# Softmax weights of an attention layer, turned by VectorE and a trip through DRAM instead of TensorE transposes

## The chip, the cores and the metric

The kernel runs on one core of one Trainium2 chip. The metric is the device time of one execution in microseconds. The engines are called as the profile calls them: PE is TensorE (matmuls; PEld is its weight load), DVE is VectorE, ACT is ScalarE, POOL is GpSimd, SP is SyncE. POOL and SP issue most DMAs here; "SPq" and "POOLq" are their DMA queues. Each engine works off its own list of instructions in order, and an instruction that has to wait holds up everything behind it on its engine.

## The reference

Two layers of a decoder run over 512 rows of 1024 floats. Layer 0 mixes the rows by dilated attention, layer 1 by a gated linear recurrence; each mixer is followed by a gated feed-forward block with a short convolution. The change touches the attention of layer 0 alone:

```
for g in range(3):              # (window, dilation): (128, 1), (512, 4), (2048, 16)
    o[g], lse[g] = dilated_group_attention(q, k, v, bias, window, dilation)
alpha = softmax(stack(lse), axis=0)
out   = sum(alpha * o) @ w_o    # 8 heads of 128 in each group

# in one group, in blocks of window // dilation positions:
logits = q @ k.T * scale + bias;  p = exp(logits - max);  o = p @ v / sum(p)
```

To multiply the weights p by v on TensorE, p has to lie with its keys on the partitions, while the softmax needs its queries there. So every block of p is turned between the two.

## The kernel before

Every product of activations and weights is done in three passes (`mm3`, line 255): each matrix is split into a rounded part and a remainder, hi x hi, hi x lo and lo x hi. ScalarE writes the rounded part of the weights (lines 143 and 149), VectorE the remainder (lines 144 and 150), up to eight units ahead of TensorE.

Attention works through the heads in pairs. For a pair, `feat_tiles` projects queries and keys one 128-column tile after the other (24 matmuls each, rows `ps L255`); for every second pair in the first half, and for every pair in the second half, `values` projects the values (rows `v L673`). Between these tiles, a call of `tick()` takes one step of whatever side work is due. The steps of a head are written as a generator: `yield n` means that the next part is put into the program n ticks later. The whole program order is fixed in this way; nothing reorders it later.

- `local(h, ...)` is the group with dilation 1, 8 heads. It loads a bias table `T` (`toeplitz`, line 586, a DMA on GpSimd), forms the scores (S, line 724), adds the bias and takes the maximum (`scores`, line 711, VectorE), takes exponentials (line 737, ScalarE), then after 2 ticks transposes 7 blocks of 128x128 on TensorE (line 746) and copies them out of PSUM (lines 749 and 751), and one tick later multiplies them by v (O, line 759).
- `strided(h, ...)` is the other two groups together, 8 heads: two tables, S at line 774, exponentials at line 789, a normalization on VectorE (line 801), then after 2 ticks eight transposes (line 808) with copies on ScalarE (line 810). A small row of factors goes through DRAM (`crow` and `cn`, lines 813 and 815). Four ticks later (five for head 6) O follows at line 821.
- `regroup` carries the sums of the first half through DRAM once (lines 835 and 837).
- The side work `biases` writes the rows from which the tables are cut (line 579) and then runs `feature_columns`: per-feature parameters of the later layers are loaded with small DMAs on GpSimd into tiles `st` (`columns`, line 485), transposed on TensorE (line 488) and copied to tiles `cols`. It has five such groups, the first with eight loads.

Tiles `L`, `PT`, `qk`, `v`, `o0`, `cn`, `st` and others come from one pool of 28 buffers of 128x512; the bias tables have two buffers.

Of the kernel before, what the change touches and what calls it, by code (L numbers as in the profile page):

```python
# [11 lines left out]
F32 = mybir.dt.float32  # L12
F32R = mybir.dt.float32r
I32 = mybir.dt.int32
AF = mybir.ActivationFunctionType
# [3 lines left out]
P = 128  # L19
# [16 lines left out]
TOE_BUFS = 2  # L36
# [38 lines left out]
def kernel(  # L75
# [25 lines left out]
    nc = tc.nc  # L101
# [5 lines left out]
    gp = ctx.enter_context(tc.tile_pool(name="gp", bufs=GEN_BUFS))  # L107
    sp = ctx.enter_context(tc.tile_pool(name="sp", bufs=8))
    pp = ctx.enter_context(tc.tile_pool(name="pp", bufs=8, space=bass.MemoryType.PSUM))
    dp = ctx.enter_context(tc.tile_pool(name="dp", bufs=1, space=bass.MemoryType.DRAM))  # L110
# [3 lines left out]
    def nm(s):  # L114
        uid[0] += 1
        return f"{s}{uid[0]}"

    def gen(dt=F32, s="g"):
        return gp.tile([P, 512], dt, tag="g", name=nm(s))

    def psum(s="ps"):
        return pp.tile([P, 512], F32, tag="ps", name=nm(s))

    def small(cols, s="s"):
        return sp.tile([P, cols], F32, tag=f"s{cols}", name=nm(s))

    mm = nc.tensor.matmul

    ident = cp.tile([P, P], F32, tag="ident", name="ident")
# [435 lines left out]
    def attention(hT, post, pre):  # L565
# [17 lines left out]
        def toeplitz(dst, g, h, n):  # L583

            o = rowv[g].offset + h * TOE + 257 - n
            nc.gpsimd.dma_start(dst, bass.AP(tensor=rowv[g].tensor, offset=o, ap=[[1, P], [1, n]]))

        vrows = []
        st0 = cp.tile([P, 4, 2, 8], F32, tag="st0", name="st0")
        o0 = []  # L590
# [116 lines left out]
        def vtile(vs, t, part):  # L707
            return vs[t][:, part * P : (part + 1) * P]

        def scores(dst, ps, bias, mx):  # L710
            nc.vector.tensor_tensor_reduce(
                dst, ps, bias[:, ::-1], scale=1.0, scalar=3 * NEG, op0=ALU.add, op1=ALU.max, accum_out=mx
            )

        def local(h, hh, q, k, v):
            T = gp.tile([P, 256], F32, tag="toe", name=nm("toe"), bufs=TOE_BUFS)
            toeplitz(T, 0, h, 256)
            L = [gen(s="L") for _ in range(2)]
            Sp = [psum("S") for _ in range(2)]
            mx = small(4)  # L720
            for a in range(4):
                o = (a % 2) * 256
                lo, k0 = (P, 0) if a == 0 else (0, (a - 1) * P)
                mm(Sp[a // 2][:, o + lo : o + 256], q[hh][:, a * P : (a + 1) * P], k[hh][:, k0 : (a + 1) * P],  # L724
                   start=True, stop=True)
            for a in range(4):
                o = (a % 2) * 256
                lo = P if a == 0 else 0
                scores(L[a // 2][:, o + lo : o + 256], Sp[a // 2][:, o + lo : o + 256], T[:, : 256 - lo], mx[:, a : a + 1])
            neg = small(4)  # L730
            nc.vector.tensor_scalar(neg, mx, -1.0, None, op0=ALU.mult)
            nc.vector.tensor_copy(st0[:, :, 0, h], mx)
            for a in range(4):
                o = (a % 2) * 256
                lo = P if a == 0 else 0
                ls = L[a // 2][:, o + lo : o + 256]
                nc.scalar.activation(ls, ls, AF.Exp, bias=neg[:, a : a + 1], accum_out=st0[:, a, 1, h : h + 1])
            yield 2
            blocks = [(a, j) for a in range(4) for j in range(2) if a or j]
            pts = {}  # L740
            for c in range(2):
                grp = blocks[4 * c : 4 * c + 4]
                ps = psum("PT")
                for n, (a, j) in enumerate(grp):
                    o = (a % 2) * 256 + j * P
                    nc.tensor.transpose(ps[:, n * P : (n + 1) * P], L[a // 2][:, o : o + P], ident)  # L746
                pt = gen(s="PT")
                if c:
                    nc.scalar.activation(pt[:, : len(grp) * P], ps[:, : len(grp) * P], AF.Copy)
                else:  # L750
                    nc.vector.tensor_copy(pt, ps)
                for n, b in enumerate(grp):
                    pts[b] = pt[:, n * P : (n + 1) * P]
            yield 1
            po = psum("O")
            for a in range(4):
                js = [1] if a == 0 else [0, 1]
                for j in js:
                    mm(po[:, a * P : (a + 1) * P], vtile(v, a - 1 + j, h % 4), pts[a, j], start=j == js[0], stop=j == 1)  # L759
            o = gen(s="o0")  # L760
            nc.scalar.activation(o, po, AF.Copy)
            o0.append(o)

        def strided(h, hh, qks, v):
            st1 = st1_box[0]
            mx = small(12)
            Ls = []
            for gi, (q, k) in enumerate(qks):
                T = gp.tile([P, 256], F32, tag="toe", name=nm("toe"), bufs=TOE_BUFS)
                toeplitz(T[:, :P], gi + 1, h, P)  # L770
                ps = psum("S")
                for r in range(4):
                    c = slice(r * P, (r + 1) * P)
                    mm(ps[:, c], q[hh][:, c], k[hh][:, c], start=True, stop=True)  # L774
                L = gen(s="L")
                for r in range(4):
                    c = slice(r * P, (r + 1) * P)
                    scores(L[:, c], ps[:, c], T[:, :P], mx[:, 4 * gi + r : 4 * gi + r + 1])
                Ls.append(L)
            M, nM, c0, den, s12 = small(4), small(4), small(4), small(4), small(8)  # L780
            nc.vector.tensor_tensor(M, mx[:, 0:4], mx[:, 4:8], op=ALU.max)
            nc.vector.tensor_tensor(M, M, st1[:, 0, h, :], op=ALU.max)
            nc.vector.tensor_scalar(nM, M, -1.0, None, op0=ALU.mult)
            nc.vector.tensor_tensor(c0, st1[:, 0, h, :], M, op=ALU.subtract)
            nc.scalar.activation(c0, c0, AF.Exp)
            for gi, L in enumerate(Ls):
                for r in range(4):
                    c = slice(r * P, (r + 1) * P)
                    nc.scalar.activation(
                        L[:, c], L[:, c], AF.Exp, bias=nM[:, r : r + 1],  # L790
                        accum_out=s12[:, 4 * gi + r : 4 * gi + r + 1],
                    )
            nc.vector.tensor_tensor(den, c0, st1[:, 1, h, :], op=ALU.mult)
            nc.vector.tensor_tensor(den, den, s12[:, 0:4], op=ALU.add)
            nc.vector.tensor_tensor(den, den, s12[:, 4:8], op=ALU.add)
            rden = small(4)
            nc.vector.reciprocal(rden, den)
            nc.vector.tensor_tensor(c0, c0, rden, op=ALU.mult)
            for L in Ls:
                L3 = L.rearrange("p (r c) -> p r c", r=4)  # L800
                nc.vector.tensor_tensor(L3, L3, rden.unsqueeze(2).to_broadcast([P, 4, P]), op=ALU.mult)
            yield 2
            pts = []
            for L in Ls:
                ps = psum("PT")
                for r in range(4):
                    c = slice(r * P, (r + 1) * P)
                    nc.tensor.transpose(ps[:, c], L[:, c], ident)  # L808
                pt = gen(s="PT")
                nc.scalar.activation(pt, ps, AF.Copy)  # L810
                pts.append(pt)
            row = dp.tile([P, 4], F32, name=f"crow{h}")
            nc.gpsimd.dma_start(row, c0)
            cn = gen(s="cn")
            nc.gpsimd.dma_start(cn, bass.AP(tensor=row.tensor, offset=row.offset, ap=[[0, P], [1, S]]))
            yield 5 if h == 6 else 4
            po = psum("O")
            for r in range(4):
                c = slice(r * P, (r + 1) * P)
                for gi in range(2):  # L820
                    mm(po[:, c], vtile(v, r, 2 * gi + hh), pts[gi][:, c], start=gi == 0, stop=gi == 1)  # L821
            r_u = "p (u r) -> p r u"
            o = o0[h]
            nc.vector.tensor_tensor(o, o, cn, op=ALU.mult)
            nc.vector.tensor_tensor(
                o.rearrange(r_u, r=4), po.rearrange("p (r u) -> p r u", r=4), o.rearrange(r_u, r=4), op=ALU.add
            )
            oT[h] = o
# [14 lines left out]
        for hp in range(4):  # L843
            q, k = [], []
            if hp % 2 == 0:
                v = []
# [9 lines left out]
        for hp in range(4):  # L856
            qs, ks, v = [], [], []
# [209 lines left out]
```

## Time and profile before

| | |
|---|---|
| median of 3 runs | 1474.26 us (1474.23 to 1474.28) |
| the profiled execution | 1474.08 us, of which the span of the profile is 1472.3 us |
| PE busy | 1463.5 us, 99% of the span |
| DVE busy | 847.1 us, 58% |
| ACT busy | 679.6 us, 46% |
| POOL busy | 43.2 us, 3% |
| DMA | 154.39 MB, 105 GB/s on average |
| attention | from the start to about 480 us |

A row of a timeline or of the chain gives the start in us from the span's start, the duration in us, the engine, the line, the operation with output and input, and how many instructions were merged (x16). What stands in brackets at the end is the idle time of the engine before it and what ended that. A row of the groups gives busy time in us and the mean of one in ns. A row of the waits gives the total in us, how often, and the longest. A row of the DMA issues gives the size and the median time from issue to landing in us. One fp32 matmul of S or O shows as two MATMUL rows, a transpose as one.

### The profile page before, as it was taken

How to read it: one execution, taken by the hardware profiler on the slowest of the kernel's cores; microseconds unless marked ns; L12 is line 12 of the kernel's file. 1: busy time of each engine (PE TensorE's matmuls, PEld its weight loads, DVE VectorE, ACT ScalarE, POOL GpSimd, SP SyncE). 2: the span in 40 equal slices, each digit the busy share in tenths (PEclk: the TensorE clock that was granted, in tenths of full speed). 3: DMA queues.
4: the chain of work that ended last, by engine and by line, in shares of the span. 5: the costliest groups of instructions: out<-in, count | busy, mean ns of one | idle time of the engine just before them, and what ended most of it. 6: DMA issues, size and time to landing. Idle time of an engine off the chain costs nothing.

```text
span 1472.3 us, 18613 instructions
## 1 busy us (share of the span) xinstructions
PE 1463.5 (99%) x7030; PEld 1231.3 (84%) x7030; DVE 847.1 (58%) x1888; ACT 679.6 (46%) x1538; POOL 43.2 (3%) x111
## 2 busy tenths in 40 slices
PE   9999999999999999999999999999999999999998
PEld 7888888888888898888888888988898888888886
DVE  5645546454545786555555337868785555565333
ACT  7645536262615454433444234489454333444321
POOL 0400001010100000000000000000000000000000
PEclk9999999999999999999999999999999999999999
DMA  6622235343434333223223231341323323223201
GB/s 203 198 65 89 91 91 140 112 137 113 127 125 130 118 115 114 87 91 110 86 106 124 86 99 44 122 138 58 110 97 108 101 86 114 87 87 129 100 0 58
DMA packets 116082, 154.39 MB, mean 105 GB/s; under 512 B 5208, under 2 KB 97592, under 8 KB 115992
## 3 DMA queue, kind: packets, MB, share of 16 engines
q1 hardware_dynamic: 112104, 144.72, 29.9%
q0 software_dynamic: 3296, 7.43, 2.5%
q8 instruction: 55, 0.90, 0.3%
q10 hardware_dynamic: 592, 1.05, 0.2%
q14 instruction: 35, 0.29, 0.1%
HBM read 146.81 MB, written 6.38 MB: 104 GB/s over the span
## 4 chain that ended last, share of the span: by engine, by line
PE 93%; ACT 4%; DVE 3%; issue 1%; DVEq 0%; ACTq 0%
PE ps L255 54%; PE acc L255 24%; PE v L673 7%; PE v L614 1%; DVE xb L879 1%; PE O L821 1%; PE S L774 1%; PE O L759 1%; PE S L724 1%; DVE wlo L150 1%; PE tr L302 1%; ACT sig L900 1%; ACT whi L149 1%; PE PT L808 0%; PE PT L746 0%
## 5 line engine op out<-in xcount | busy, mean ns | idle before, releaser
L255 PE MATMUL ps<-hT,whi 128*128 128x512 f32 (+1 forms) x2752 | 801.6, 375 | 0.0
L255 PEld LDWEIGHTS ps<-hT,whi 128*128 128x128 f32 x2752 | 503.2, 188 | 91.0
L255 PE MATMUL ps<-hT,wlo 128*128 128x512 f32 (+1 forms) x1376 | 515.2, 374 | 0.0
L150 DVE TENSOR_TENSOR wlo<-raw,whi 128x512 fp32r<-128x512 f32 x360 | 230.8, 686 | 190.1 <-ACT whi L149 190.1
L255 PEld LDWEIGHTS ps<-hT,wlo 128*128 128x128 f32 x1376 | 259.1, 188 | 46.5
L149 ACT ACTIVATE whi<-raw 128x512 fp32r<-128x512 f32 x360 | 204.7, 622 | 135.3 <-PE acc L255 120.9
L538 DVE SCALAR_TENSOR_TENSOR u<-ps,cols,u 128x511 f32<-128x511 f32 x192 | 143.8, 749 | 139.9 <-ACT u L534 136.5
L255 PE MATMUL acc<-whi,ahi 128*128 128x512 f32 x512 | 199.9, 390 | 0.0
L255 PE MATMUL acc<-whi,alo 128*128 128x512 f32 x512 | 199.4, 389 | 0.1
L255 PE MATMUL acc<-wlo,ahi 128*128 128x512 f32 x512 | 199.2, 389 | 0.0
L143 ACT ACTIVATE whi<-raw,first_w 128x128 fp32r<-128x128 f32 (+1 forms) x432 | 146.5, 427 | 62.4 <-PE ps L255 53.2
L534 ACT ACTIVATE u<-ps,cols 128x512 f32<-128x512 f32 x96 | 74.8, 779 | 209.3 <-PE ps L255 209.3
L144 DVE SCALAR_TENSOR_TENSOR wlo<-raw,first_w,whi 128x128 fp32r<-128x128 f32 (+1 forms) x432 | 141.9, 391 | 37.5 <-ACT whi L143 37.5
L255 PEld LDWEIGHTS acc<-whi,alo 128*128 128x128 f32 x512 | 96.1, 188 | 20.3 <-DVE alo L150 0.6
L255 PEld LDWEIGHTS acc<-wlo,ahi 128*128 128x128 f32 x512 | 96.2, 188 | 19.9
L255 PEld LDWEIGHTS acc<-whi,ahi 128*128 128x128 f32 x512 | 96.2, 188 | 19.7
L673 PE MATMUL v<-whi,hT 128*128 128x512 f32 x320 | 103.6, 395 | 0.0
L673 PEld LDWEIGHTS v<-whi,hT 128*128 128x128 f32 x320 | 60.1, 188 | 12.1
L549 ACT ACTIVATE u<-u 128x512 f32<-128x512 f32 x48 | 30.3, 632 | 81.2 <-DVE u L538 81.2
L673 PE MATMUL v<-wlo,hT 128*128 128x512 f32 x160 | 62.3, 390 | 0.0
L353 DVE TENSOR_TENSOR post<-acc,gain 128x512 f32<-128x512 f32 x32 | 22.0, 686 | 46.5 <-ACT junk L262 46.5
L601 DVE TENSOR_TENSOR qk<-ps,roots 128x512 f32<-128x512 f32 x24 | 16.6, 690 | 53.4 <-PE ps L255 53.4
(163 smaller groups left out, 969.2 us busy)
## 6 DMA issues: line engine op xcount, KB each, us to landing
raw<-in_ffn_w_up_dram SPq DMA_DIRECT2D x48, 1024.0 KB, 5.2
raw<-in_attn_w_qkv_dram SPq DMA_DIRECT2D x26, 1024.0 KB, 5.0
raw<-in_ffn_w_down_dram SPq DMA_DIRECT2D x24, 1024.0 KB, 5.0
raw<-in_attn_w_qkv_dram SPq DMA_DIRECT2D x19, 512.0 KB, 6.7
raw<-in_lru_w_in_dram SPq DMA_DIRECT2D x8, 1024.0 KB, 5.4
vrows<-v SPq DMA_DIRECT2D x16, 256.0 KB, 3.8
vp<-vrows SPq DMA_DIRECT2D x16, 256.0 KB, 3.7
raw<-in_attn_w_o_dram SPq DMA_DIRECT2D x4, 1024.0 KB, 5.0
```

What stands on the lines that cost most here:

```text
L143: nc.scalar.activation(hi[:, k], raw[:, k], AF.Copy, scale=w)
L144: nc.vector.scalar_tensor_tensor(lo[:, k], raw[:, k], w, hi[:, k].bitcast(F32), op0=ALU.mult, op1=ALU.subtract)
L149: nc.scalar.activation(hi, raw, AF.Copy)
L150: nc.vector.tensor_tensor(lo, raw, hi.bitcast(F32), op=ALU.subtract)
L255: mm(dst, l[a], r[b], start=start and n == 0, stop=stop and n == 2)
L302: nc.tensor.transpose(ps[:, k * P : (k + 1) * P], xs[i][:, k * P : (k + 1) * P], ident)
L353: nc.vector.tensor_tensor(u[i], parts[i], g[:, at[i]], op=ALU.mult)
L534: nc.scalar.activation(u, ps, AF.Identity, scale=cc[:, j : j + 1], bias=cc[:, 48 + j : 49 + j])
L538: nc.vector.scalar_tensor_tensor(u[:, d:], ps[:, : S - d], wc, u[:, d:], op0=ALU.mult, op1=ALU.add)
L549: nc.scalar.activation(u, u, AF.Gelu_apprx_tanh)
L601: nc.vector.tensor_tensor(dst, src, row, op=ALU.mult)
L673: mm(banks[t], hT[a][:, k, t * P : (t + 1) * P], W[b][:, k % 2, :], start=(k, a, b) == (0, 0, 0), stop=(k, a, b) == (KD - 1, 1, 0),)
```

## The change

The transposes on TensorE, their PSUM tiles and their copies are taken out of both `local` and `strided`. In their place `turned` lets VectorE turn each 32x32 block of `L` where it is (one instruction for 3 or 4 blocks of 128x128) and writes the result to a DRAM tile; `fetched` reads it back with four DMAs, one for each group of 32 partitions, so that each 32x32 block arrives at its place in the full transpose. The columns of the fetched tile come in another order, so O reads its moving operand as four runs of 32. All these DMAs are issued by GpSimd. Per head there are two turned tiles, two writes and eight fetches.

The steps are put elsewhere too. The turning and the trip are now in the same part as the exponentials, ahead of the `yield`; O follows 4 ticks after S in `local` (3 before) and 6 in `strided` (7 for head 6), as before. `table` asks for a bias table one head ahead, and a `strided` head has both of its tables in one tile.

```
+        def table(strided, h, take=True):
+            if (strided, h) not in tables:
+                T = gp.tile([P, 256], F32, tag="toe", name=nm("toe"), bufs=TOE_BUFS)
+                for i in range(1 + strided):
+                    n = 256 >> strided
+                    toeplitz(T[:, i * n : i * n + n], i + strided, h, n)
+                tables[strided, h] = T
+            return tables.pop((strided, h)) if take else None

+        def turned(L, n, name, first=0):
+            T = gen(s="T")
+            nc.vector.transpose(
+                T[:, : n * P].rearrange("p (c n j) -> p c n j", c=4, j=32),
+                L[:, first * P : (first + n) * P].rearrange("p (n c j) -> p c n j", c=4, j=32),
+            )
+            d = dp.tile([P, n * P], F32, name=nm(name))
+            nc.gpsimd.dma_start(d, T[:, : n * P])
+            return d

+        def fetched(d, n):
+            pt = gen(s="PT")[:, : n * P]
+            for c in range(4):
+                nc.gpsimd.dma_start(
+                    pt[32 * c : 32 * c + 32].rearrange("j (b x) -> j b x", b=4),
+                    d.rearrange("(b j) (c x) -> c j b x", j=32, c=4)[c],
+                )
+            pt = pt.rearrange("p (b n i) -> p n b i", b=4, i=32)
+            return [pt[:, i] for i in range(n)]

         def local(h, hh, q, k, v):
-            T = gp.tile([P, 256], F32, tag="toe", name=nm("toe"), bufs=TOE_BUFS)
-            toeplitz(T, 0, h, 256)
+            T = table(0, h)
...
                 nc.scalar.activation(ls, ls, AF.Exp, bias=neg[:, a : a + 1], accum_out=st0[:, a, 1, h : h + 1])
-            yield 2
+            table(*((0, h + 1) if h < 7 else (1, 0)), False)
+            ds = [turned(L[c], 4 - (c == 0), "ptl", int(c == 0)) for c in range(2)]
             blocks = [(a, j) for a in range(4) for j in range(2) if a or j]
-            pts = {}
-            for c in range(2):
-                grp = blocks[4 * c : 4 * c + 4]
-                ps = psum("PT")
-                for n, (a, j) in enumerate(grp):
-                    o = (a % 2) * 256 + j * P
-                    nc.tensor.transpose(ps[:, n * P : (n + 1) * P], L[a // 2][:, o : o + P], ident)
-                pt = gen(s="PT")
-                if c:
-                    nc.scalar.activation(pt[:, : len(grp) * P], ps[:, : len(grp) * P], AF.Copy)
-                else:
-                    nc.vector.tensor_copy(pt, ps)
-                for n, b in enumerate(grp):
-                    pts[b] = pt[:, n * P : (n + 1) * P]
-            yield 1
+            pts = dict(zip(blocks, fetched(ds[0], 3) + fetched(ds[1], 4)))
+            yield 4
             po = psum("O")
...
         def strided(h, hh, qks, v):
+            T = table(1, h)
             for gi, (q, k) in enumerate(qks):
-                T = gp.tile([P, 256], F32, tag="toe", name=nm("toe"), bufs=TOE_BUFS)
-                toeplitz(T[:, :P], gi + 1, h, P)
...
-            yield 2
-            pts = []
-            for L in Ls:
-                ps = psum("PT")
-                for r in range(4):
-                    c = slice(r * P, (r + 1) * P)
-                    nc.tensor.transpose(ps[:, c], L[:, c], ident)
-                pt = gen(s="PT")
-                nc.scalar.activation(pt, ps, AF.Copy)
-                pts.append(pt)
+            if h < 7:
+                table(1, h + 1, False)
+            ds = [turned(L, 4, "pts") for L in Ls]
             row = dp.tile([P, 4], F32, name=f"crow{h}")
             nc.gpsimd.dma_start(row, c0)
+            pts = [fetched(d, 4) for d in ds]
             cn = gen(s="cn")
             nc.gpsimd.dma_start(cn, bass.AP(tensor=row.tensor, offset=row.offset, ap=[[0, P], [1, S]]))
-            yield 5 if h == 6 else 4
+            yield 7 if h == 6 else 6
...
-                    mm(po[:, c], vtile(v, r, 2 * gi + hh), pts[gi][:, c], start=gi == 0, stop=gi == 1)
+                    mm(po[:, c], vtile(v, r, 2 * gi + hh), pts[gi][r], start=gi == 0, stop=gi == 1)
```

In the changed file the lines of `local` and `strided` stand some lines further down: S is at 757 and 794, O at 780 and 835, the turning at 730, the write at 735 and the fetch at 742; `toeplitz`, `columns` and `mm3` keep theirs.

More of the change, by code (lines that the diff above doesn't have):

```diff
@@ L586, in toeplitz @@
             nc.gpsimd.dma_start(dst, bass.AP(tensor=rowv[g].tensor, offset=o, ap=[[1, P], [1, n]]))
+        tables = {}
+        def table(strided, h, take=True):
[6 more added lines that the diff above has]
+            return tables.pop((strided, h)) if take else None
         vrows = []
@@ L777, in strided @@
                     c = slice(r * P, (r + 1) * P)
-                    scores(L[:, c], ps[:, c], T[:, :P], mx[:, 4 * gi + r : 4 * gi + r + 1])
+                    scores(L[:, c], ps[:, c], T[:, gi * P : gi * P + P], mx[:, 4 * gi + r : 4 * gi + r + 1])
                 Ls.append(L)
```

## The prediction

> **What bounds the kernel now.** I read the page first, then what TensorE waited for, then the chain of waits in the attention stretch, and last the timelines of GpSimd and ScalarE around the one place where the changed order of instructions looked dangerous.
>
> ```profile
> span 1472.3 us, 18613 instructions
> PE 1463.5 (99%) x7030; PEld 1231.3 (84%) x7030; DVE 847.1 (58%) x1888; ACT 679.6 (46%) x1538; POOL 43.2 (3%) x111
> PEclk9999999999999999999999999999999999999999
> PE 93%; ACT 4%; DVE 3%; issue 1%; DVEq 0%; ACTq 0%
> ```
> ```profile
> PE warm L995 <- DVE one L1027: 1.5, 1, 1.5
> ```
>
> TensorE (PE) is busy 99% of the span and 93% of the chain that ends last. The second fence is the longest of its waits in the view; the others it lists are of 0.2 us. So two things count: TensorE work that is taken out comes off the end, and a wait that TensorE is given is paid in full, because no slack follows it. VectorE (58%) and ScalarE (46%) have room.
>
> **What is removed.** The chain's pieces show what the transposes hold on TensorE's path.
>
> ```profile
> 74.31 0.20 PE cols L488
> 74.51 0.91 PE PT L746 x7
> ...
> 82.66 0.76 PE PT L746 x7
> ...
> 237.62 0.87 PE PT L808 x8
> ```
>
> The 56 transposes of `local` (8 heads of 7) are eight pieces, the first of 0.91 and seven like the second row, 0.76 to 0.77: 6.3 us. The 64 of `strided` (8 heads of 8) are eight pieces like the third row, 0.87 or 0.88: 7.0 us. The gain on the path is 13.3 us. The copies out of PSUM that go with them, 24 on ScalarE and 8 on VectorE, are off the path, since nothing on TensorE waits for them above 0.2 us; I count them at nothing.
>
> **What VectorE gets.** 32 block transposes of 384 or 512 columns. No trace row shows one. The nearest are a 128x512 copy and, as the slow end, the add that writes every fourth element:
>
> ```profile
> L751 DVE COPY PT<-PT 128x512 f32<-128x512 f32 x8 | 5.5, 688 | 15.2 <-PE PT L746 15.2
> L825 DVE TENSOR_TENSOR o<-O,o 128x512 f32<-128x512 f32 x8 | 8.6, 1069 | 5.5 <-PE O L821 5.4
> ```
> ```profile
> 65.48 1.42 DVE L144 SCALAR_TENSOR_TENSOR wlo<-raw,first_w,whi 128x512 fp32r<-128x512 f32 x2 [2.58 <-ACT whi L143]
> ```
>
> I take 0.65 us, next to the copy's 0.69 (1069 ns is the other end), since runs of 32 elements stay contiguous. In `local` the new pass must wait for the exponentials, and VectorE's queue behind it holds the weight splits of L144; but those wait for the same stretch of ScalarE today (2.58 us idle), so the pass falls into idle time. In `strided` it follows VectorE's own normalization and adds 1.3 us per head, under eight weight units split ahead. Cost on the path: none. Without that cover it would be 32 x 0.65 - 5.5 = 15 us; at 1069 ns, 29 us.
>
> **What GpSimd gets, and what it is queued ahead of.** This decides the sign. Each head now issues two writes to DRAM and eight fetches on GpSimd's queue, in order. In the built program of the changed kernel GpSimd's order is: table of head 0, table of head 1, the ten DMAs of head 0, table of head 2, the ten of head 1, and only then the L485 loads of `columns`. On TensorE the place of the first L488 transpose, which needs eight of those loads, is unchanged. Before, the loads went out early:
>
> ```profile
> 48.99 2.02 POOL L485 DMA_DIRECT2D st<-in_lru_conv_w_dram  x4
> ...
> 52.48 0.50 POOL L485 DMA_DIRECT2D st<-in_lru_lambda_dram  x1
> ```
>
> They were out at 53 us and TensorE asked at 74.3: over 20 us of lead. Now they stand behind two trips that cannot start until heads 0 and 1 have their exponentials:
>
> ```profile
> 63.66 0.18 ACT L737 ACTIVATION_READ_ACCUMULATOR L<-L,s 128x1 f32 x1
> 64.65 0.18 ACT L737 ACTIVATION_READ_ACCUMULATOR L<-L,s 128x1 f32 x1
> 71.66 0.18 ACT L737 ACTIVATION_READ_ACCUMULATOR L<-L,s 128x1 f32 x1
> ```
> ```profile
> vrows<-v SPq DMA_DIRECT2D x16, 256.0 KB, 3.8
> cn<-crow POOLq DMA_DIRECT2D x8, 256.0 KB, 4.5
> toe<-rowv POOLq DMA_DIRECT2D x16, 64.0 KB, 3.1
> crow<-s POOLq DMA_DIRECT2D x8, 2.0 KB, 1.9
> st<-in_lru_conv_w_dram POOLq DMA_DIRECT2D x4, 4.0 KB, 2.4
> st<-in_lru_conv_b_dram POOLq DMA_DIRECT2D x1, 4.0 KB, 5.3
> st<-in_lru_lambda_dram POOLq DMA_DIRECT2D x1, 4.0 KB, 4.4
> L586 POOL DMA_DIRECT2D toe<-rowv x24 | 12.9, 539 | 290.1 <-DVE s L711 198.3 <-DVE st L732 90.4 <-DVE s L781 1.4
> L835 POOL DMA_DIRECT2D strows<-st x1 | 0.8, 772 | 31.3 <-ACT L L737 31.3
> ```
> ```profile
> 453.66 0.54 POOL L813 DMA_DIRECT2D crow<-s  x1 [4.06 <-DVE s L798]
> 455.86 0.54 POOL L815 DMA_DIRECT2D cn<-crow  x1 [1.66 <-DMA crow<-s]
> ```
>
> A 256 KB write on GpSimd's queue isn't in the trace. `vrows` has its size and direction (3.8), `cn` its size and queue (4.5); I take the middle, 4.15, with ends 1.9 (`crow`) and 4.5. The next issue comes 2.2 us after `crow` where 1.9 is the landing: 0.3 more. An issue of 128 strips takes 0.54 (L586), and a fetch has 128 strips; the end above is 0.77 (L835, 512 strips).
>
> On the clock of the profile before: head 0's first half has its exponentials at 63.8, is turned at 64.4 and issued. It is back for reading at 64.4 + 4.15 + 0.3 = 68.85; the second half, written at 65.5, is ready under the first four fetches. Eight fetches of 0.54 end at 73.2, the table at 73.7. Head 1 was turned by 71.84 + 0.65 = 72.5, so its writes wait for the queue: issued 73.7 and 74.2. Its first half is ready at 78.15, its fetches end at 82.5. Eight column loads of 0.50 follow; the last issues at 86.0 and lands 4.4 later, at 90.4. TensorE stands at L488 from 74.3 to 90.4: **16.1 us**, once. The other column loads follow on at 0.5 us and are there when asked, one and two tiles later.
>
> By the Trainium skill, page "DMA: Bandwidth & Descriptors", section "Anatomy of one DMA — SWDGE (gpsimd) path", a DMA issued by GpSimd takes about 2.0 us plus its bytes over 436 GB/s, so an estimate of 2.5 us for the 192 KB write and 2.0 for a column load: a stop of about 10 us instead of 16.1, and 1472.5 us for the whole. Its 2.2 us for 64 KB stands against a measured 3.1, its 2.6 us for 256 KB against 4.5, so the rows decide.
>
> **What the stop does to the rate behind it.** The trace shows TensorE after a rest only at the start:
>
> ```profile
> 1.47 2.50 PE L995 MATMUL warm<-one 128*128 128x512 f32 x5 [1.47 <-DVE one L1027]
> 4.87 1.48 PE L995 MATMUL warm<-one 128*128 128x512 f32 x3
> 7.47 1.00 PE L614 MATMUL v<-wlo,hT 128*128 128x512 f32 x2
> 10.62 1.07 PE L614 MATMUL v<-whi,hT 128*128 128x512 f32 x4
> ```
>
> Five matmuls in 2.50 us are 0.53 apart (less 0.39 for the last one's length), four in 1.07 us are 0.23: half rate, although the PEclk row says 9 there. From 4.87 to the end of the third row TensorE worked 3.6 us almost unbroken and stayed slow; half of that is lost, **1.8 us**. Ends: 0, if a rest in mid-run does nothing, and 3.4, half of 1.47 to 8.3. The Trainium skill, "TensorE: Matmul & The Clock Gate", Part 1, states the rule against any such stop: after an idle window of about 3.4 us the clock is halved until a window of work has passed, 1.7 us lost as an estimate; the start-up rows agree, and no run shows it after a mid-kernel stop.
>
> **Edits at nothing.** The tables are asked for earlier, but no score waits for one (L711's releaser in the groups is the S matmul), so nothing is gained. The O matmuls of `local` come one tick later, those of `strided` at the same tick. They now read 4 runs of 32 columns; no matmul in the trace reads its moving side so, and I count no cost. The trips move 448 KB per `local` and 512 KB per `strided` head each way, some 15 MB over 400 us, 38 GB/s. The tightest trip is head 7's:
>
> ```profile
> 453.25 1.78 PE S L774 x16
> ...
> 478.64 3.57 PE O L821 x32
> 463.17 1.28 DVE L801 TENSOR_TENSOR L<-L,s 128x512 f32<-128x512 f32 x2
> ```
>
> Head 7's weights are normalized 11.2 us after its S began (464.45). Two transposes of head 6 ahead and one of its own make 13.1; written and readable at 17.5; eight fetches issued by 21.8, the last landing at 24.4. Its O comes, without the transposes, 25.4 - 1.75 + 1.78 = 25.4 us after S. The margin is 1 us: nothing now, up to 3 us if landing or issuing is slower.
>
> **The sum.** -13.3 + 16.1 + 1.8 = +4.6 us. Against the profiled execution (1472.3 us of span, 1474.08 in all) that is 1478.7; the median of the runs is 0.18 above that execution, so the forecast is **1478.9**. About 0.2% (2.9 us) is what a measurement of this kernel can tell from no change; +4.6 is 0.31%.
>
> **The rivals.**
> - *Short trips: faster or no change.* Small transfers on this queue land in 1.9 and 2.4 us. With these, head 0's fetches end at 70.6, head 1's writes wait for its own exponentials (the second at 72.5, the first 1.1 earlier, as in head 0), its fetches end at 77.6, the last load issues at 81.1 and lands at 83.5. The stop is 9.2 us: 1470.2 without a slow restart, 1472.0 with it. It becomes a gain when the stop and its restart are under 13.3. The skill's DMA rule above would give about this case. Against it: every 64 to 256 KB transfer took 3.1 to 4.5, and of the loads the four later ones 4.4 to 5.3. Chance 0.2, of which 0.09 passes 0.2%.
> - *GpSimd's queue becomes the bound.* At 0.77 an issue 16 fetches before the loads cost 3.7 us more, at 4.5 and 5.3 us the landings 1.6 more: a stop of 21.4, a restart of 3.4, and heads 6 and 7 late by 3: +14.5, 1488.8. It shows where an O matmul waits for PT. For it: the queue is in order and the margin is 1 us; against: 0.54 for 128 strips is steady over 24 issues. Chance 0.22.
> - *Broken-up reads slow the O matmuls.* The add with broken-up access takes 1069 ns against the copy's 688. The 240 passes of the O matmuls (112 and 128), 0.111 us each by the 478.64 row, at that ratio would cost 15 us: 1494. Chance 0.05, since runs of 128 bytes are left.
> - *The change does what it says but nothing waits*, 1461.0: only if the column loads were ahead in GpSimd's queue, and the built order has them behind. Chance 0.02.
>
> **How the numbers follow.** The forecast, a stop of 13 to 19 us with a short restart, has 0.51 and runs from 1476 to 1482. Of it 0.15 lies within 0.2%, together with 0.11 of the short trips: same 0.26. Faster: 0.09, the other part of the short trips with the last rival inside it. Slower: 0.65. The range goes from 1472.5, inside the short trips, to 1489.0, the queue rival.
>
> **What would show it.** Right: TensorE's waits of after have one entry of 13 to 19 us at L488, released by the loads into `st`, and GpSimd shows the L485 rows after 80 us; the first matmuls behind it stand 0.4 to 0.5 us apart; elsewhere attention is shorter by 0.76 or 0.87 per head. Wrong: no wait at L488, waits of TensorE at the O matmuls (L780, L835) in many heads, block transposes over 1.1 us with splits late behind them, or fetches that occupy GpSimd for over 0.8 us.

## The result, and the profile after

The changed kernel takes 1485.37 us in the median (1484.73 to 1486.44, 4 runs) against 1474.26 (1474.23 to 1474.28) before: the ratio is 1.0076, with a 95% interval of 1.0064 to 1.0088. It is slower by 11.1 us, 0.8%. The forecast was 1478.9, on the right side and 6.5 us too low. The profiled execution took 1486.44 us, 12.4 more than the profiled one of before; all sums below are made against these two.

The page of the changed kernel, the same lines as before:

```profile
span 1484.7 us, 18710 instructions
PE 1456.8 (98%) x6910; PEld 1223.1 (82%) x6910; DVE 860.3 (58%) x1912; ACT 669.7 (45%) x1514; POOL 131.5 (9%) x271
PEclk9989999999999899999999999999999999999999
PE 82%; ACT 5%; issue 5%; DVE 4%; DMA 3%; POOL 1%; DVEq 0%; ACTq 0%; POOLq 0%
```

TensorE has 120 instructions less, as the change says. Its share of the chain that ends last fell from 93% to 82%, and in two slices the granted clock has a dip where the row of before was flat. The waits of TensorE say where (total, times, longest, in us):

```profile
PE cols L488 <- DMA st<-in_lru_lambda_dram: 14.1, 1, 14.1
PE O L835 <- DMA PT<-pts: 4.8, 2, 2.8
PE O L835 <- DMA vp<-vrows: 0.4, 1, 0.4
```

There are two stops: the one at the first column transpose, which was forecast, and one at an O near the end of attention, which was not.

**The first stop.** The chain that ended last, from 74 us on:

```profile
74.74 1.09 DMA ptl<-T
75.84 2.79 issue
78.62 1.40 POOL PT L742 x3
...
83.00 3.50 POOL st L485 x7
86.50 1.64 DMA st<-in_lru_lambda_dram
88.14 0.30 issue
88.44 0.34 PE cols L488
88.78 7.72 PE ps L255 x24
```

Read from below: TensorE goes on at 88.44 because the eighth column load has landed. That load was issued at 86.50, behind seven others on GpSimd's queue, which had begun at 83.00, behind the fetches of head 1, which had begun at 78.62, behind its own writes. For the 2.79 us called `issue` the profile names no releaser; in the program the fetches have to wait there for these writes to land. It is the round trip of another head that stands ahead of the loads. Behind the stop, the next tile of 24 matmuls takes 7.72 us, where the same tile takes 5.6 at full rate (experiment 3).

**The second stop.** TensorE's timeline around the O matmuls of heads 6 and 7 in the second half, and GpSimd's before it (start, duration; in brackets the idle time ahead and its end):

```profile
481.48 1.50 PE L835 MATMUL O<-PT,vp 128*128 128x128 f32 x12
483.38 0.71 PE L835 MATMUL O<-PT,vp 128*128 128x128 f32 x4 [0.40 <-DMA vp<-vrows]
486.90 0.76 PE L835 MATMUL O<-PT,vp 128*128 128x128 f32 x2 [2.82 <-DMA PT<-pts]
489.68 3.33 PE L835 MATMUL O<-PT,vp 128*128 128x128 f32 x14 [2.01 <-DMA PT<-pts]
```
```profile
471.69 1.09 POOL L735 DMA_DIRECT2D pts<-T  x2
472.77 0.54 POOL L826 DMA_DIRECT2D crow<-s  x1
476.99 4.38 POOL L742 DMA_DIRECT2D PT<-pts  x8 [3.68 <-issue]
```

Head 7's last fetch is issued by 481.4 and is still awaited at 489.7, 8 us later. The same stretch in windows (PE busy, PEld, DVE, ACT, POOL; then the granted clock, the DMA engines' share, and GB/s):

```profile
480.00:485.00 5.00, 3.69 (x24) 3.03 (x22) 1.93 (x3) 0.00 (x0) 1.94 (x4) 1.00 1.02 272
485.00:490.00 5.00, 1.08 (x3) 0.85 (x4) 0.18 (x1) 0.63 (x1) 0.00 (x0) 0.56 1.08 298
490.00:495.00 5.00, 5.00 (x20) 4.52 (x20) 2.48 (x4) 0.63 (x1) 0.00 (x0) 0.50 0.93 321
```

The DMA engines are full from 480 to 490 while TensorE waits, and behind the wait its clock is granted at half. This slows the O matmuls themselves: the 14 rows from 489.68 to 492.66 are 0.21 us apart, where the 12 rows in one piece at 481.48 are 0.11 apart.

**The sum, from one tile's start to the same tile's start in both traces.** The first stop with its neighbours puts TensorE 14.2 us behind, the half-rate tile another 2.1; the block without transposes takes back 6.3 in the first half and 7.0 in the second; the O of the last pair takes 11.2 us (481.48 to 492.66) where 3.5 was due, 7.7 too many, of which 5.2 are waits and 2.5 slow or broken-up matmuls, and the slow matmuls behind it cost 1.5. That is 14.2 + 2.1 - 6.3 - 7.0 + 7.7 + 1.5 = 12.2, and from 513 us on the two traces run in parallel, 12.2 us apart.

### The profile page after: what moved, and what is told of

Same layout as the page of the kernel before. It is cut to its first block, busy times and chain, and to the rows that moved or that the text cites. A ratio compares the mean times of both kernels' runs of the same rounds, so it can differ in the third digit from the quotient of the medians.

```text
span 1484.7 us, 18710 instructions
## 1 busy us (share of the span) xinstructions
PE 1456.8 (98%) x6910; PEld 1223.1 (82%) x6910; DVE 860.3 (58%) x1912; ACT 669.7 (45%) x1514; POOL 131.5 (9%) x271
## 3 DMA queue, kind: packets, MB, share of 16 engines
q10 hardware_dynamic: 592, 1.05, 0.2%
## 4 chain that ended last, share of the span: by engine, by line
PE 82%; ACT 5%; issue 5%; DVE 4%; DMA 3%; POOL 1%; DVEq 0%; ACTq 0%; POOLq 0%
PE ps L255 49%; PE acc L255 23%; PE v L685 6%; DMA PT<-pts 1%; ACT whi L143 1%; DVE xb L893 1%; DMA raw<-in_attn_w_qkv_dram 1%; PE O L780 1%; PE v L626 1%; DVE wlo L150 1%; DVE wlo L144 1%; PE S L794 1%; PE tr L302 1%; PE O L835 1%; ACT sig L914 1%
## 5 line engine op out<-in xcount | busy, mean ns | idle before, releaser
L685 PEld LDWEIGHTS v<-whi,hT 128*128 128x128 f32 x320 | 60.1, 188 | 12.2
```

Source lines behind the costliest of these rows:

```text
L685: mm(banks[t], hT[a][:, k, t * P : (t + 1) * P], W[b][:, k % 2, :], start=(k, a, b) == (0, 0, 0), stop=(k, a, b) == (KD - 1, 1, 0),)
```

## The experiments

Beside each of them the kernel before was run on the same chip, with a median of 1474.1 us every time.

**1. The column loads first.** All column loads are issued right behind the first two tables, ahead of any trip.

```
+                if g == 2:
+                    table(0, 0, False)
+                    table(0, 1, False)
+                    load_columns()          # the DMAs of L485, all five groups
...
-            nc.gpsimd.dma_start(st[at : at + c, :P], src)
+        st = loaded.pop(0)
```

> The column loads are issued on GpSimd right behind the first two bias tables, ahead of all trips, as in the kernel before; everything else is the changed kernel. Theory (the stop at the first column transpose, 14.1 us, and the slow tile behind it, 2.1 us, come from the place of these loads in GpSimd's queue): both go, 1485.4 - 16.3 = 1469 us, with the wait at heads 6 and 7 left. Rival (the trips load GpSimd's queue as such, and the stop only shows where it surfaces first): other waits of TensorE come up in the first half, and the time stays over 1475.

Measured: 1469.47 us (1468.04 to 1470.54, 7 runs), ratio 0.9969 (0.9958 to 0.998). The wait at `cols` is gone; of waits at O, this is the longest row:

```profile
PE O L853 <- DMA PT<-pts: 6.1, 2, 5.0
```

No other wait came up in the first half, as the rival would have it. Against the changed kernel it is 15.9 us, which is about the stop and its slow tile (14.1 + 2.1). One moved block of issues turns the sign of the whole change.

**2. The last pair on TensorE again.** Only heads 6 and 7 of the second half are transposed as before.

```
+            if h >= 6:
+                yield 2
...             # transposes on TensorE and copies on ScalarE, as before
+            else:
+                ds = [turned(L, 4, "pts") for L in Ls]
...
-            yield 7 if h == 6 else 6
+            yield (7 if h == 6 else 6) - 2 * (h >= 6)
```

> Heads 6 and 7 of the second half are transposed on TensorE again, as in the kernel before; all other heads make the trip. Theory (the last trip is late and costs 7.7 us of stop and 1.5 us of slow matmuls behind it): this goes and 1.75 us of transposes come back: 1485.4 - 9.2 + 1.8 = 1478. Rival (the DMA engines are full there whatever the weights do, and O waits for the values as well): O still waits for the values' DMA, over 1483.

Measured: 1477.79 us (1477.25 to 1478.81, 9 runs), ratio 1.0025 (1.0015 to 1.0035). This is 7.6 us under the changed kernel, about the tail's 9.2 (7.7 + 1.5) less the 1.8 that 16 transposes cost. The first stop alone is left:

```profile
PE cols L488 <- DMA st<-in_lru_lambda_dram: 13.3, 1, 13.3
```

That the time lies within 1.1 us of the forecast is in part luck: 1.8 us of transposes are back, which the forecast had removed, and the stop is 2.8 us shorter than forecast.

**3. TensorE kept busy through the first stop.** Sixty matmuls that nobody reads are put ahead of the first column transpose.

```
+        if n == 64:
+            fill = psum("fill")
+            for _ in range(60):
+                mm(fill, first_hT[0][:, 0, :P], first_hT[0][:, 0, :], start=True, stop=True)
```

> The changed kernel with 60 matmuls of 128x512 (13.7 us of TensorE work that nothing reads) put ahead of the first column transpose, where TensorE stands for 14.1 us. Theory (the tile behind the stop takes 7.6 us and not 5.5 because TensorE rested): the tile takes 5.5, the time falls by 2.1 to 1483.3. Rival (it is slow because its weights were split late or because memory is busy): the tile still takes 7.6 and the time is unchanged at 1485.4.

Measured: 1484.27 us (1483.91 to 1485.41, 4 runs), ratio 1.007 (1.0055 to 1.0085). TensorE's timeline behind the fill, and below it the same place in the changed kernel:

```profile
74.18 13.76 PE L490 MATMUL fill<-hT 128*128 128x512 f32 x60
89.27 0.24 PE L492 MATMUL cols<-ident,st 64*128 64x64 f32 x1 [1.33 <-DMA st<-in_lru_gx_b_dram]
89.45 0.73 PE L255 MATMUL ps<-hT,whi 128*128 128x512 f32 x2
90.01 0.39 PE L255 MATMUL ps<-hT,wlo 128*128 128x512 f32 x1
90.24 0.62 PE L255 MATMUL ps<-hT,whi 128*128 128x512 f32 x2
```
```profile
88.71 1.22 PE L255 MATMUL ps<-hT,whi 128*128 128x512 f32 x2
89.72 0.63 PE L255 MATMUL ps<-hT,wlo 128*128 128x512 f32 x1
90.15 1.05 PE L255 MATMUL ps<-hT,whi 128*128 128x512 f32 x2
```

With the fill, a pair ends in 0.62 us; after the rest, in 1.05. The tile behind takes 5.6 us (89.45 to the next `cols` at 95.03) and not 7.72. So the slow tile comes from the rest, as stated. That the time fell by 1.1 us and not by 2.1 doesn't come from the fill, which had ended 1.33 us before the column transpose: the loads landed later in this execution, so that the transpose came at 89.27 and not 88.44. The runs of the two kernels also overlap, so the tile's own rows, and not the 1.1 us, carry the finding. The Trainium skill, "TensorE: Matmul & The Clock Gate", Part 1, says that the clock is halved after an idle window of about 3.4 us until a busy window has passed. The first stop, of 14.1 us, agrees, with 2.1 us lost behind it. The second shows more than the rule gives: none of its waits is over 2.82 us, and the windows above still grant 0.56 and then 0.50, with up to 2.5 us lost among the O matmuls and 1.5 behind them.

**4. The gain rows earlier.** Two loads of 512 KB, which SyncE issues at 478 us, are asked for some 35 us earlier, to take them out of the second stop's stretch.

```
+            if hp == 3:
+                gains.extend([gain(*post, nc.sync), gain(*pre, nc.sync)])
```

> The two gain rows of 512 KB each, which SyncE asks for at 478 us amid the last trips, are asked for some 35 us earlier, right behind the last query and key tile; all else is the changed kernel. Theory A (the last fetches are late because the DMA engines are full from 480 to 495 us, at 272 to 321 GB/s): 1 MB less there at about 300 GB/s is 3.5 us, so 1482 or a little less, and the wait of O at heads 6 and 7 shrinks by as much. Theory B (the trip is too long by itself, two landings and eight issues in a row): no change, 1485.4.

Measured: 1485.67 us (1484.59 to 1486.56, 4 runs), ratio 1.008 (1.0063 to 1.0097): no change. The wait at O is still 4.8 us and the engines are as full:

```profile
485.00:490.00 5.00, 1.74 (x6) 1.51 (x7) 0.00 (x0) 0.29 (x1) 0.00 (x0) 0.60 1.08 304
490.00:495.00 5.00, 5.00 (x23) 4.49 (x23) 3.06 (x4) 0.63 (x1) 0.00 (x0) 0.72 0.23 73
```

Theory A failed in this form. The window that became empty is the one behind the fetches (0.23 where it was 0.93). SyncE's next weight loads moved up into the place of the gain rows: two of them are issued from 476.95 to 479.13, where the changed kernel issued the second at 480.76. So the fetches had as much traffic beside them as before, and this run doesn't tell whether traffic was what delayed them.

**5. Experiments 1 and 2 together.**

> Column loads ahead of the trips, and heads 6 and 7 of the second half transposed on TensorE: the two repairs together. Theory (all the loss lies in these two waits, block transposes, longer GpSimd queue and broken-up reads of O cost nothing): TensorE waits for nothing after the start, and 104 of 120 transposes are gone, 13.3 - 1.8 = 11.5 us: 1474.1 - 11.5 = 1462.6. Rival (the traffic of the trips also costs elsewhere): waits for weights appear and the time stays over 1465.

Measured: 1462.59 us (1462.53 to 1462.63, 4 runs), ratio 0.9921 (0.9904 to 0.9937). Beside the 1.5 us at the very start, which every version has, this is the only wait of TensorE in the view, and the profile before has it too:

```profile
PE v L644 <- ACT hT L316: 0.2, 1, 0.2
```

11.5 us are gained, the 13.3 of the transposes less the 1.8 of the pair that is back. So the removed transposes are worth what was forecast, and VectorE's block transposes, the broken-up reads and 14 heads' trips cost nothing on the path.

**6. The same, with each bias table asked for in its own head.**

```
-            table(*((0, h + 1) if h < 7 else (1, 0)), False)
...
-            if h < 7:
-                table(1, h + 1, False)
```

> As the kernel with both repairs, but each bias table is asked for in its own head, as before the change. Theory (asking one head ahead gained nothing by itself, but in GpSimd's ordered queue the table of a pair's second head would stand behind the first head's whole trip, some 15 to 20 us): VectorE waits that long for the table at the scores of every odd head, and since weight splits queue behind, TensorE loses a few us per pair: 1467 to 1490. Rival (the table is needed late enough, or splits are far enough ahead): VectorE waits but TensorE doesn't, 1462.6.

Measured: 1485.45 us (1482.41 to 1487.23, 4 runs), ratio 1.0074 (1.0059 to 1.0089): 22.9 us are lost. GpSimd's timeline in the second half, and VectorE's at the head that waits:

```profile
231.28 1.14 POOL L753 DMA_DIRECT2D pts<-T  x2 [25.86 <-DVE T L748]
...
242.21 1.09 POOL L604 DMA_DIRECT2D toe<-rowv  x2
```
```profile
246.51 0.29 DVE L741 CUSTOM_DVE_ANT_0 L<-S,toe 128x128 f32<-128x128 f32 x1 [12.86 <-DMA toe<-rowv]
```

The tables of the second head of a pair stand behind the whole trip of the first, and VectorE stands 12.86 us for them. In the whole execution VectorE waits 37.6 us for tables, where it waits for none in experiment 5. Without the trips the tables had needed no lead; with them, the lead is what keeps the scores going. How the 22.9 us divide on TensorE's path wasn't worked out: its waits behind the start come to 12 us in the profiled execution, all at O matmuls, for the values' rows, for ScalarE and, in 2.9 us of it, for nothing that the profile names.

**7. The next stage's weight loads held during the last trips.** On top of experiment 1, the loads of the next weights are put into the program behind the O of heads 6 and 7.

```
-            while not pieces and state["dma"] < len(plan) and ...
+            while not state["still"] and not pieces and state["dma"] < len(plan) and ...
...
+            if h == 6:
+                state["still"] = True
             yield 7 if h == 6 else 6
+            if h == 7:
+                state["still"] = False
```

> Column loads ahead of the trips, all heads on the trip, and the 1 MB weight loads of the next stage held back while the trips of heads 6 and 7 are under way (3 MB less beside them). Theory A (the last fetches land late because the DMA engines are shared with these loads): the fetches land in 3 to 4 us instead of 8, the wait of O, 6.1 us, and the slow restart, 1.5 us, go: 1469.5 - 7.6 = 1462. Theory B (the trip is too long by itself, or the values' own DMAs are what it shares with): O waits as before, 1469.5.

Measured: 1467.39 us (1465.83 to 1468.22, 4 runs), ratio 0.9952 (0.9937 to 0.9967), 2.1 us under experiment 1, between the two theories. A place in the program is not a place in time: SyncE doesn't wait for an O, so it issued the loads at once, from 460.30 on, while TensorE came to this O at 465.13.

**8. The same with the gain rows early.**

> As the last one, and the two gain rows are asked for before the last trips too, so that beside these only the values (1 MB each way) and the trips themselves are moved. Theory A: as the last one or a little better, 1461 to 1462. Theory B: no change, 1469.5. If it is the gains behind the held loads that matter, this one alone is fast.

Measured: 1466.7 us (1466.21 to 1467.54, 4 runs), ratio 0.9949 (0.9934 to 0.9964). Little more. SyncE's timeline shows what the hold did, and TensorE's what was left:

```profile
459.30 33.03 SPq L199 DMA_DIRECT2D raw<-in_ffn_w_up_dram  x4
```
```profile
465.07 1.95 PE L859 MATMUL O<-PT,vp 128*128 128x128 f32 x16
468.30 0.46 PE L859 MATMUL O<-PT,vp 128*128 128x128 f32 x2 [1.28 <-DMA PT<-pts]
471.41 2.31 PE L859 MATMUL O<-PT,vp 128*128 128x128 f32 x14 [2.65 <-DMA PT<-pts]
```

The first of these weight loads (1 MB each) is issued at 459.30, among the fetches, which GpSimd issues from 458.55 to 462.92.

**9. The weight loads behind the fetches in time.** Four small reads of head 7's fetched weights are put on SyncE's queue ahead of the held loads, so that the queue has to wait for the fetches.

```
             if h == 7:
                 state["still"] = False
+                for r in range(4):
+                    nc.sync.dma_start(dp.tile([1, P], F32, name=f"seen{r}"), pts[1][0][32 * r : 32 * r + 1, :])
```

> The kernel with the column loads first, the gain rows early and the weight loads held, with one thing more: four reads of 512 bytes from head 7's fetched weights into DRAM, on SyncE's queue ahead of the held weight loads, so that these are not issued until the last fetch has landed. Theory A (the late landing of the last pair's fetches is sharing with the next stage's weight loads, which in the two runs with held loads still ran beside them): the fetches land about 4 us after their issue instead of 8.7, TensorE's wait at O falls from 3.9 us to under 0.5, and the time from 1466.7 to about 1462.7 (the value with head 7's pair on TensorE and the column loads first was 1462.6), if the weights, asked some 10 us later, still come in time for the stage behind. Theory B (the late landing is with the fetches themselves, 128 strips to each of many transfers, and with the values' rows): O's wait stays 3 to 4 us and the time stays 1466.7 or rises, by what the later weights cost.

Measured: 1461.16 us (1461.11 to 1461.52, 4 runs), ratio 0.9913 (0.9896 to 0.9929), theory A. SyncE's and TensorE's timelines:

```profile
465.07 2.50 SPq L856 DMA_DIRECT2D seen<-PT  x4
467.61 28.85 SPq L199 DMA_DIRECT2D raw<-in_ffn_w_up_dram  x5
```
```profile
465.16 3.73 PE L861 MATMUL O<-PT,vp 128*128 128x128 f32 x32
```

All 32 rows of O now run in one piece, and TensorE waits for none of the weight loads, which come 8.3 us later than in experiment 8. The views of the tile `PT` (from 445 us, or in the changed kernel from 460 us, to behind the O), one row of each, give the time from issue to landing of the last pair's 16 fetches: first the changed kernel, then experiment 8, then 9.

```profile
DMA to landing us min/median/max: 4.7/6.9/9.0
```
```profile
DMA to landing us min/median/max: 2.1/3.6/9.5
```
```profile
DMA to landing us min/median/max: 2.1/3.2/5.0
```

Beside the weight loads a fetch of 64 KB takes up to 9.0 or 9.5 us; with them out of the way the slowest takes 5.0. The Trainium skill, "DMA: Bandwidth & Descriptors", section "Queues, rings and completion order", says that each DMA engine takes the queues it has work for in turn, packet by packet. The pair of experiments 8 and 9 agrees with sharing of this kind: GpSimd's fetches are on another queue than SyncE's loads, and the slowest landed in 9.5 us beside these and in 5.0 without. The order in which packets were taken, no run here shows.

This version beats both kernels: 13.0 us (0.9%) under the one before, 24.2 under the changed one.

## Why the prediction was right or wrong, point by point

**What bounds the kernel; the transposes, -13.3: right.** 5 and 9 gave 11.5 (of 11.5 due) and 13.0 us.

**VectorE's block transposes at nothing: right.** The groups of the changed kernel:

```profile
L730 DVE STREAM_TRANSPOSE T<-L 128x512 f32<-128x512 f32 x24 | 16.1, 695 | 3.3 <-ACT L L770 3.3
L742 POOL DMA_DIRECT2D PT<-pts x64 | 35.0, 555 | 26.9 <-issue 13.4 <-ACT whi L143 10.9 <-DMA pts<-T 2.6
L780 PE MATMUL O<-PT,v 128*128 128x128 f32 x112 | 13.8, 275 | 0.0
```

695 ns stand against 0.65 us and the copy's 688. Nothing on TensorE waits for one.

**An issue of 128 strips, 0.54: right**, at 0.555 over 64 issues. The queue rival's 0.77 was not seen as a mean, only in single issues, of up to 0.81. **Broken-up reads at nothing: right.** The O of `local` takes 275 ns a row, as it did before the change.

**The stop at the first column transpose, 16.1: the mechanism right, the size 2.0 too large.** GpSimd's steps ended where they were worked out to end: the fetches of head 1 began at 78.62 (78.15 stated), the last load was issued at 86.50 (86.0). That they did so within 0.5 us is in part luck. Head 0's first write was issued at 65.83 and not 64.4, but its fetches could begin 2.8 us later and not 4.45; then GpSimd stood 1.03 us for a landing ahead of the next table, which the sum doesn't have:

```profile
68.60 4.42 POOL L742 DMA_DIRECT2D PT<-ptl  x8 [1.09 <-DMA ptl<-T]
74.04 0.57 POOL L586 DMA_DIRECT2D toe<-rowv  x1 [1.03 <-DMA PT<-ptl]
```

The term that was mis-sized is the landing of the last load, 1.64 us where 4.4 was taken from the row of `lambda` before. The load of before ran at another time and beside other traffic; which of these made it slower wasn't tested. The estimate of 2.0 by the Trainium skill's "DMA: Bandwidth & Descriptors", section "Anatomy of one DMA — SWDGE (gpsimd) path", was the nearer for this load, but the stop of about 10 us that goes with it was 4 too short, in part because head 1's fetches began 3.9 us after its first write was issued, where that estimate has 2.5 for the write.

**The slow restart, 1.8: right**, 2.1 measured, and experiment 3 shows that the rest causes it.

**Head 7's trip, "nothing now, up to 3 us": wrong, and this is more than the whole miss.** The prediction worked with a last landing 24.4 us after S and a margin of 1. The issues were late by 1.7 us (fetches issued by 23.5 after S began at 457.9, not 21.8), and the last landing came at about 31.6. The step that failed is the fetch's landing, 2.6 us assumed behind the last issue and about 8 measured. It agrees with the 64 KB row of the bias tables less the issue, 3.1 - 0.54, a median over the whole kernel, and was used at a place where, as the windows show, the DMA engines are full. The cost was 9.2 us against a bound of 3: 5.2 of waits, 2.5 of slow matmuls within O and 1.5 behind it. The forecast has no restart at this stop. The miss of 7.7 us (1486.44 against 1478.7) is made of -2.0, +0.3 and +9.2, and 0.2 of small waits.

**The rivals.** The queue rival's time, 1488.8, lies nearer to the measured one than the forecast does, and its sign "an O matmul waits for PT" was there. Its mechanism, slow issues, was not: the delay was in the landing. "Short trips" was right on the landing of the column loads (1.64 us for the last one) and wrong on the trips: the last load was issued at 86.50 and not 81.1, and the stop was 14.1 us and not 9.2. Its sum also leaves out the 0.3 us that the main sum puts behind a write. "Nothing waits", 1461.0, is what the change is worth once its two stops are removed: experiment 9 gave 1461.16. The chance of "slower", 0.65, is 0.02 more than its cases add up to (0.36 + 0.22 + 0.05).

**Tables one head ahead at nothing: right for what was asked, and incomplete.** No score waited for a table before, so the lead gains nothing by itself; experiment 6 shows that the trips make it necessary, and that without it 22.9 us go.

**What stays open.** In experiment 9 the values' own rows still travel beside the last fetches, and the slowest fetch still takes 5.0 us against a least of 2.1. What part of that is theirs was not measured, as no wait hangs on it.

## What to carry to other kernels

When work goes from a busy engine into DMAs, list everything that stands on the issuing queue behind the new trip, tables and parameters of later stages too, and move what can start earlier ahead of it: here that order alone was worth 15.9 us, more than the transposes. A landing time holds for the traffic of the place that it was read from, so a tight trip has to be priced with the DMA share of its own window, and bulk loads on other queues may have to be held back by a real dependency, since a later place in the program delays nothing on a queue that waits for nobody. Each stop of the busy engine is to be charged with its half-rate restart as well, here 2.1 us at the first and up to 4.0 at the second.

## What the runs showed of the hardware that was not expected

A 64 KB fetch of 128 strips landed in 2.1 us at best and in 9.5 at worst, in the same stretch of one execution (experiment 8). A 4 KB load landed in 1.64 us where its row before said 4.4. TensorE's granted clock fell to 0.56 and 0.50 at the second stop, whose waits were of 0.40, 2.82 and 2.01 us with work between them; how short a stop may be to do this, no run shows. Writes of 256 KB from GpSimd's queue, bounded between 1.9 and 4.5 us beforehand, took 2.6 in the first half and 4.7 in the second, as these two rows of the DMA issues of the changed kernel say:

```profile
pts<-T POOLq DMA_DIRECT2D x16, 256.0 KB, 4.7
ptl<-T POOLq DMA_DIRECT2D x8, 256.0 KB, 2.6
```
